# Expert weights in runs of 16 KB per partition: a changed order of features and hidden units in a mixture-of-experts kernel

## The chip, the cores and the metric

One core of one Trainium2 chip runs the whole program. The metric is the time of one execution on the device in microseconds (us); before the change it is 1592.47 us, the median of three runs.

## What is computed

256 tokens of 1024 features go through two blocks. The first mixes tokens (a recurrent RWKV half and an attention half), adds the result to its input, normalises the sum and sends every token to 4 of 32 experts. The second block mixes again and ends in a plain feed-forward network. The change is in the expert layer and in what feeds it; cut to that, the reference is:

```python
x = x + gate1 * (concat([y_rwkv, y_moba]) @ w_out)
h = rms_norm(x, norm2_g) * (1.0 + scale2) + shift2
logits = h @ w_router + b_router
top_val, top_idx = lax.top_k(logits, TOP_K)
weights = softmax(top_val)
...
gu = xb @ w_gate_up[e] + b_gate_up[e]
gate = jnp.minimum(gu[:, :D_FF], SWIGLU_LIMIT)
up = jnp.clip(gu[:, D_FF:], -SWIGLU_LIMIT, SWIGLU_LIMIT)
act = (up + 1.0) * gate * jax.nn.sigmoid(SWIGLU_ALPHA * gate)
y = act @ w_down[e] + b_down[e]
...
x = x + gate2 * segment_sum(y * weight, token)
```

`xb` are the tokens of expert `e`. All of it is float32. An expert's weights are 1024 x 2048 (`w_gate_up`) and 1024 x 1024 (`w_down`) numbers, 12.58 MB; the 32 experts have 403 MB of the 505 MB that the kernel moves. Both products sum over an index, the feature in the first and the hidden unit in the second, and a sum can be taken in any order of its index as long as both factors have the same order.

## The kernel before

**The stream of weights.** All large weights come through one DMA queue, SyncE's (SP), in chunks of 2 MB: one DMA each, into a slot of 128 partitions x 16 KB (`stream`, L105). `issue` (L1021) sends an expert's six chunks, four of `w_gate_up` and two of `w_down`, in the order of use. There are nine slots (three in `ring`, two lent to the first block at first, two each in `ring2` and `ring3`), so a chunk can be sent when the one nine places ahead of it has been used up. In a gate-and-up chunk a partition holds rows `p` and `128 + p` of a pair of groups of 128 features, two runs of 8 KB; in a down chunk it holds four rows, four runs of 4 KB.

**An expert.** `gather` (L1066) makes the input of two experts at a time with 32 products of `xm`, the sum after attention, and a one-hot matrix: `xe[:, k]` holds features `128k` to `128k + 127` on its 128 partitions, 64 slots for tokens per expert. `gate_up` (L1104) runs 32 products of 512 columns (L1117, into `pg` and `pu`), with the 64 tokens as the stationary operand and the weights as the moving one. Four VectorE operations and one of ScalarE (L1120 to L1124) then make `act` (tile `u`): 128 partitions (64 tokens, two halves of the hidden units) x 512. `down` (L1127) transposes `act` in four blocks of 128 columns on TensorE (L1133, tile `at`; the block of `act` is the stationary operand), ScalarE copies the result (L1134), and 16 products (L1139, `py`) multiply it with the down weights. Between the last product of `gate_up` and the first of `down` TensorE has nothing else to do in the experts but for pieces of `gather`, of `combine` (L1149, tile `cb`) and biases that the scheduler put there.

**Ahead of the experts.** `phase1` loads the router's weights `wr` (L593), makes the columns `sc2` and `sh2` (the gain and the shift of the norm's output, feature by feature) from rows `r1` by the four small products of `ada_col` (L293, tile `adac`) and three VectorE operations (L597 to L599), adds what the shift is worth to the router's bias (L602) and folds the gain into `wr` (L604, GpSimd). When the last products with `w_out` are done, the sum `xm` is made in four pieces of 512 features (L871 and L872: two halves `a` of the tokens, two halves `c` of the features), `choose` (L888) transposes it (L897, tile `x1t`), computes the logits (L906) and the mask, `rank` (L919) places the tokens in the experts' slots, and GpSimd copies `xm` to `x1` (L880), the running sum to which the experts add.

The order of instructions on each engine is a scheduler's, made from the program's order and its own costs; it can move an instruction when another one's shape changes.

Of the kernel before, what the change touches and what calls it, by code (L numbers as in the profile page):

```python
# [15 lines left out]
OP = mybir.AluOpType  # L16
# [7 lines left out]
# plain PSUM banks before the experts; buffers of the RWKV and of the stick-breaking attention; how many experts  # L24
# before the last one the memory tokens come in
NP, B4, NZ, ME = 4, 5, 5, 12

# columns of the packed per-feature vectors
# [14 lines left out]
# columns of the constants (they depend on shapes alone)  # L43
# [48 lines left out]
class Kernel:  # L92
# [11 lines left out]
    # ---- weights stream: one order, one queue, a ring of slots  # L104
# [8 lines left out]
    def split(self, pool, src, n, name, eng):  # L113
        """src = hi + lo exactly, each in float32r"""
        hi = pool.tile([128, n], F32R, tag=name + "h", name=name + "h")
        lo = pool.tile([128, n], F32R, tag=name + "l", name=name + "l")
        self.nc.scalar.activation(hi, src, AF.Copy)  # L117
        eng.tensor_tensor(lo, src, hi.bitcast(F32), op=OP.subtract)  # L118
        return hi, lo
# [21 lines left out]
    def setup(self):  # L141
# [9 lines left out]
        # what is not needed past the experts  # L151
        self.xe = ExitStack()
        cp = self.pool("cpe", es=self.xe)
        # x after the attention, its scale per token, and the norm's gain and shift with the modulation, per feature
# [28 lines left out]
    def rsqrt(self, out, src, eps=None, scale=1.0, refine=None):  # L183
        """(src * scale + eps) ** -0.5; with a pool to take temporaries from, one Newton step more"""
# [25 lines left out]
    # ================================================================ first block, before the experts  # L210
    def expert_bias(self, pool):
        """the gate and up biases as three exact bfloat16 parts, on 3 x 32 partitions"""
# [11 lines left out]
    def phase1(self):  # L224
# [9 lines left out]
        # ---- modulation rows: silu(c) @ w_ada + b_ada; the i-th 512 columns add up on the partitions i mod 32  # L234
# [7 lines left out]
        # two slots of the stream that are at first lent to the RWKV and the MoBA  # L242
# [24 lines left out]
        def gate_rows():  # L267
            """rows 4, 5, 10 and 11, for the gates: partition by partition, the bias on one of them"""
# [14 lines left out]
        def gate_bc(q):  # L283
            """a row of a gate on every partition"""
# [4 lines left out]
        def ada_col(r, i0):  # L289
            """rows i0..i0+3 as columns [feature, (row, 128 features)]"""  # L290
# [6 lines left out]
        # ---- x over its root mean square, transposed  # L297
# [29 lines left out]
        # ---- h = rms(x) * g1 * (1 + scale1) + shift1, transposed, as hi + lo  # L327
# [19 lines left out]
        # ---- projections  # L347
# [10 lines left out]
        def dense_T(src, ncols, tiles, consume):  # L358
            """features on partitions; tiles: (first column, columns) of the chunk; two to a bank"""
# [13 lines left out]
        def dense_N(src, consume, then=lambda: None):  # L373
            """tokens on partitions, 512 columns"""
# [21 lines left out]
        def shift_mix(dst, ps, m, mi):  # L396
            """p + (shift(p) - p) * mu"""
# [45 lines left out]
        # ---- RWKV, element by element: decays inside chunks of 64 steps, scaled keys and receptances  # L443
# [9 lines left out]
        for g in ((0, 2), (2, 4)):  # L453
# [3 lines left out]
            # k * k_k over its norm per head  # L457
# [10 lines left out]
            # k * (1 + (a - 1) * k_a)  # L468
# [18 lines left out]
        # ---- RWKV, chunk by chunk: two chunks of 64 steps side by side, eight heads  # L487
# [10 lines left out]
        def pairs(lhs, rhs, tt, name):  # L498
            """per head, [step of lhs, step of rhs]; even heads, then odd ones"""
# [8 lines left out]
        def sub(s):  # L508
            """superchunk s: everything that needs neither the inverse nor the state"""
# [11 lines left out]
            # (I - L)^T of every 16 steps, kept as [row, head, column of the block]  # L521
# [4 lines left out]
        def invert(s, r):  # L526
            """(I - L)^T of every 16 steps: column r times row r of L^T goes to the columns after r"""
# [22 lines left out]
        # ---- MoBA projections (one block, so plain causal attention with ALiBi)  # L550
# [38 lines left out]
        # ---- the router's weights with the gain and the scale of its input folded in, and what its shift adds  # L589
        wr = p1.tile([128, 8, NE], F32, tag="wr", name="wr")  # L590
        cvec = self.W[:, 0]
        with tc.issue_after(self.last_dma):
            nc.sync.dma_start(wr, A["w_router"].rearrange("(k p) e -> p k e", p=128))  # L593
            nc.sync.dma_start(cvec, A["b_router"].partition_broadcast(128))
        pv = ada_col(r1, 6)
        sc2, sh2 = self.sc2, self.sh2
        DVE.tensor_scalar(ic(sc2), pv[:, 2:4], 1.0, None, op0=OP.add)  # L597
        DVE.tensor_tensor(sc2, sc2, self.v("g2"), op=OP.mult)
        DVE.tensor_copy(ic(sh2), pv[:, 0:2])  # L599
# [12 lines left out]
        def sub2(s):  # L612
# [3 lines left out]
            for n, src in (("v", vT), ("a", aT), ("b", bT), ("k", ktT)):  # L616
                if n in ("b", "k"):
                    # decayed to the end of the chunk
# [24 lines left out]
            # what values and keys of the same chunk add to outputs and states  # L643
# [54 lines left out]
        for s in range(2):  # L698
# [32 lines left out]
            # receptance with the decayed keys' corrections folded in; outputs that the state has no part in  # L731
# [17 lines left out]
        # ---- MoBA attention, head by head  # L749
# [21 lines left out]
        def moba_out(hd):  # L771
# [4 lines left out]
            # [key, query]: keys 0..127 for all queries, then keys 128..255 for the last 128  # L776
# [20 lines left out]
        # ---- from here on the stream has more room  # L797
# [10 lines left out]
        # ---- normalised per head, bonus, gate  # L808
        eN = ExitStack()
        pc = right("pc", eN)  # L810
        for s in range(2):
# [11 lines left out]
            # meanwhile what it is multiplied by, and what is added  # L823
# [13 lines left out]
        # ---- x + (y @ w_out) * gate1  # L837
        po = [[self.psum("wo") for _ in range(2)] for _ in range(2)]

        def w_out(ks):  # L840
            """a k after the other; of the last two the first tokens first"""
# [742 lines left out]
```

## Time and profile before

| what | value |
|---|---|
| runs | 1592.47, 1597.8, 1590.65 us (median 1592.47) |
| profiled execution: span | 1590.6 us |
| profiled execution: own time | not given apart; the span lies 1.9 us below the median of the runs |
| TensorE (PE) busy | 1449.3 us, 91% |
| VectorE (DVE), ScalarE (ACT), GpSimd (POOL) busy | 37%, 25%, 13% |
| DMA | 505.15 MB in 115061 packets |
| experts: first product to last | 284 to about 1255 us of the span |

The page gives busy time per engine; the stage views give the same for stretches of the span, with the clock that the throttle granted to TensorE (PEclk, 1.00 is 2.4 GHz and 0.5 is 1.2 GHz), the mean busy share of 16 DMA engines (which can come out a little over 1) and GB/s. A timeline row has start, duration, engine, line, operation, tile written <- tiles read, shape, and in brackets the idle time before it with what ended it. SPq is the DMA queue of SyncE: a duration there is that of issuing, not of the transfer.

### The profile page before, as it was taken

What the parts mean: (1) busy time and instruction counts of PE and PEld (TensorE: products, weight loads), DVE (VectorE), ACT (ScalarE), POOL (GpSimd) and SP (SyncE); (2) the same over time, 40 slices, a digit from 0 to 9 for tenths busy, and PEclk for the clock granted to TensorE, in tenths of its full rate; (3) what the DMA queues carried; (4) which work ended last, traced back from release to release, by engine and by line L of the source; (5) the groups of instructions that cost most, each with busy time, mean ns of one, the idle gap of its engine ahead of it and who ended that gap; (6) DMA issues with size and microseconds to landing.
All of it is one profiled execution on the core that took longest, in us unless ns stands there. A gap on an engine that the chain in (4) does not pass through costs nothing. (4 is left out here: it accounts for less than half of the span.)

```text
span 1590.6 us, 19145 instructions
## 1 busy us (share of the span) xinstructions
PE 1449.3 (91%) x7818; PEld 813.4 (51%) x7818; DVE 591.2 (37%) x1177; ACT 395.1 (25%) x767; POOL 212.6 (13%) x190
## 2 busy tenths in 40 slices
PE   5999998999999989988998989999989899899996
PEld 2976876333333323323333334433333497699995
DVE  2576877232122222221222122222221345555455
ACT  4862344110000000000001011110010366455553
POOL 1243751000000000000000000000000233252221
PEclk9999999999999999999999999999999999989998
DMA  9734747899999999999999997999999451535540
GB/s 337 251 120 170 280 170 288 340 417 416 418 416 416 418 418 415 419 418 415 418 418 415 397 409 319 411 416 416 418 417 414 154 208 54 195 123 180 191 159 27
DMA packets 115061, 505.15 MB, mean 318 GB/s; under 512 B 5548, under 2 KB 6572, under 8 KB 82168
## 3 DMA queue, kind: packets, MB, share of 16 engines
q1 hardware_dynamic: 114792, 503.74, 79.9%
q8 instruction: 63, 1.03, 0.3%
q14 instruction: 30, 0.25, 0.0%
q0 software_dynamic: 176, 0.14, 0.0%
HBM read 502.81 MB, written 1.05 MB: 317 GB/s over the span
## 5 line engine op out<-in xcount | busy, mean ns | idle before, releaser
L1139 PE MATMUL py<-w,at 128*64 128x512 f32 x1024 | 265.0, 669 | 22.0 <-ACT at L1134 21.8
L1117 PE MATMUL pg<-w,xe 128*64 128x512 f32 x1024 | 267.7, 598 | 0.0
L1117 PE MATMUL pu<-w,xe 128*64 128x512 f32 x1024 | 264.9, 592 | 0.0
L1121 ACT ACTIVATE sg<-g 128x512 f32<-128x512 f32 (+1 forms) x33 | 20.2, 616 | 601.6 <-DVE g L1120 601.6
L1139 PEld LDWEIGHTS py<-w,at 128*64 128x64 f32 x1024 | 77.4, 153 | 175.7 <-issue 141.6
L1146 DVE TENSOR_TENSOR y<-py,gate 64x512 f32<-64x512 f32 x64 | 44.1, 688 | 304.4 <-PE py L1139 303.7
L1117 PEld LDWEIGHTS pu<-w,xe 128*64 128x64 f32 x1024 | 74.1, 137 | 146.7 <-issue 146.6
L117 ACT ACTIVATE w3h<-w 128x512 fp32r<-128x512 f32 x184 | 115.2, 631 | 109.1 <-PE d L1275 57.6
L1117 PEld LDWEIGHTS pg<-w,xe 128*64 128x64 f32 x1024 | 70.9, 137 | 135.0 <-issue 130.2
L118 DVE TENSOR_TENSOR w3l<-w,w3h 128x512 fp32r<-128x512 f32 x132 | 94.2, 719 | 115.7 <-ACT w3h L117 111.0
L1120 DVE TENSOR_SCALAR g<-pg 128x512 f32<-128x512 f32 (+1 forms) x33 | 22.2, 675 | 295.4 <-PE pg L1117 295.4
L118 POOL TENSOR_TENSOR w3l<-w,w3h 128x512 fp32r<-128x512 f32 x52 | 67.4, 1301 | 432.1 <-ACT w3h L117 420.9
L1274 PE MATMUL d<-xh,w3h 128*128 128x256 f32 x352 | 100.5, 288 | 0.9 <-ACT xh L1261 0.9
L1210 POOL TENSOR_TENSOR wml<-w,wml 128x512 fp32r<-128x512 f32 x4 | 5.2, 1293 | 718.5 <-ACT wml L1209 718.5
L1275 PE MATMUL d<-xl,w3h 128*128 128x256 f32 x352 | 100.8, 287 | 0.1
L1276 PE MATMUL d<-xh,w3l 128*128 128x256 f32 x352 | 100.2, 286 | 0.0
L1133 PE MATMUL at<-ca,u 128*128 128x128 f32 x128 | 23.5, 313 | 63.8 <-DVE u L1124 63.8
L1083 PEld LDWEIGHTS ga<-s,xm 128*128 128x128 f32 x512 | 62.3, 197 | 28.2 <-issue 26.5
L1083 PE MATMUL ga<-s,xm 128*128 128x128 f32 x512 | 69.8, 288 | 1.2 <-DVE s L1073 1.2
L1274 PEld LDWEIGHTS d<-xh,w3h 128*128 128x128 f32 x352 | 68.4, 196 | 1.6 <-ACT xh L1261 1.3
L1275 PEld LDWEIGHTS d<-xl,w3h 128*128 128x128 f32 x352 | 68.4, 194 | 0.9 <-DVE xl L1263 0.6
L1276 PEld LDWEIGHTS d<-xh,w3l 128*128 128x128 f32 x352 | 68.2, 194 | 0.0
(421 smaller groups left out, 2100.6 us busy)
## 6 DMA issues: line engine op xcount, KB each, us to landing
w<-w_gate_up SPq DMA_DIRECT2D x128, 2048.0 KB, 16.7
w<-w_down SPq DMA_DIRECT2D x71, 2048.0 KB, 17.6
w<-w_ada SPq DMA_DIRECT2D x12, 2048.0 KB, 9.2
w<-w_up SPq DMA_DIRECT2D x8, 2048.0 KB, 7.5
w<-w_in SPq DMA_DIRECT2D x6, 2048.0 KB, 11.4
w<-w_in_sb SPq DMA_DIRECT2D x5, 2048.0 KB, 10.3
w<-w_out SPq DMA_DIRECT2D x4, 2048.0 KB, 7.7
w<-w_mem_kv SPq DMA_DIRECT2D x1, 2048.0 KB, 12.0
```

Of the source, the lines that this page charges most:

```text
L117: self.nc.scalar.activation(hi, src, AF.Copy)
L118: eng.tensor_tensor(lo, src, hi.bitcast(F32), op=OP.subtract)
L1083: PE.matmul(ps[:, k * 128:(k + 1) * 128], xm[:, a, (kk + k) * 128:(kk + k + 1) * 128], s[:, a], start=a == 0, stop=a == 1, skip_group_chec ...
L1117: PE.matmul(p[64 * h:64 * h + 64, :], xe[:, k], w[:, k % 2, c:c + 512], start=False, stop=k == 7)
L1120: DVE.tensor_scalar(g[:, c], pg[:, c], 7.0, None, op0=OP.min)
L1121: ACT.activation(s[:, c], g[:, c], AF.Sigmoid, scale=1.702)
L1133: PE.transpose(ps[:, j * 128:(j + 1) * 128], act[:, j * 128:(j + 1) * 128], ident)
L1139: PE.matmul(py[64 * h:64 * h + 64, :], at[:, j, c], ws[c][:, j, h * 512:(h + 1) * 512], start=c == 0 and j == 0, stop=c == 1 and j == 3)
L1146: DVE.tensor_tensor(st[e & ~1][2][r, hs], py[64 * h:64 * h + 64], self.gate2[64 * h:64 * h + 64, hs], op=OP.mult)
L1274: PE.matmul(o, wh[:, ws], xh[:, k], start=k == 0 and i % 2 == 0, stop=False, skip_group_check=True)
L1275: PE.matmul(o, wh[:, ws], xl[:, k], start=False, stop=False, skip_group_check=True)
L1276: PE.matmul(o, wl[:, ws], xh[:, k], start=False, stop=k == 7, skip_group_check=True)
```

## The change

1. **Weights.** A chunk of `w_gate_up` now holds, on partition `p`, two whole groups of the rows `8p` to `8p + 7`: feature `8p + k` stands where feature `128k + p` stood, and the two rows of a chunk are neighbours in memory, one run of 16 KB. A chunk of `w_down` holds on partition `p` the rows `4p` to `4p + 3` of its half, one run of 16 KB.
2. **Features.** All that is multiplied with these rows follows: the router's weights `wr`, the columns `sc2` and `sh2` (16 products of 64 x 2 with every eighth column of `r1` as the stationary operand, in place of four of 128 x 4; the norm's gain comes by a DMA of its own), and `xm`, which VectorE now writes with a step of 512 bytes between neighbours. GpSimd undoes the order when it copies `xm` to `x1`. Each half `c` of the features now has columns in all eight blocks of `xm`.
3. **Hidden units.** The four transposes of an expert read every fourth column of `act`, a step of 16 bytes, in place of 128 neighbours. For the last expert, which works in two parts, the elementwise operations are strided too.
4. **The path for an overfull expert** (`overflow`), which isn't taken in these runs, is addressed anew.

The rest of the diff takes out comments.

```diff
         with tc.issue_after(self.last_dma):
-            nc.sync.dma_start(wr, A["w_router"].rearrange("(k p) e -> p k e", p=128))
+            nc.sync.dma_start(wr, A["w_router"].rearrange("(p k) e -> p k e", p=128))
+            nc.sync.dma_start(sc2, A["norm2_g"].rearrange("(p k) -> p k", p=128))
             nc.sync.dma_start(cvec, A["b_router"].partition_broadcast(128))
-        pv = ada_col(r1, 6)
-        sc2, sh2 = self.sc2, self.sh2
-        DVE.tensor_scalar(ic(sc2), pv[:, 2:4], 1.0, None, op0=OP.add)
-        DVE.tensor_tensor(sc2, sc2, self.v("g2"), op=OP.mult)
-        DVE.tensor_copy(ic(sh2), pv[:, 0:2])
+
+        ps = self.psum("adac")
+        for i in range(2):
+            for k in range(8):
+                PE.matmul(ps[64 * i:64 * i + 64, 2 * k:2 * k + 2], r1[:, k:512:8], self.k("sel32")[:, 6 + i:10:2],
+                          start=True, stop=True, skip_group_check=True)
+        pv = ps[:, 0:16].rearrange("p (k i) -> p i k", i=2)
+        DVE.scalar_tensor_tensor(sc2, pv[:, 1], 1.0, sc2, op0=OP.add, op1=OP.mult)
+        DVE.tensor_copy(sh2, pv[:, 0])
...
+        pk = lambda t: t.rearrange("t (p k) -> t p k", k=8)
+        xp = lambda a: xm[:, a].rearrange("t (k p) -> t p k", k=8)
         for a in range(2):
             for c in range(2):
...
-                DVE.tensor_tensor(xm[:, a, cs], x1[:, a, cs], t, op=OP.add)
+                DVE.tensor_tensor(xp(a)[:, 64 * c:64 * c + 64], pk(x1[:, a, cs]), pk(t), op=OP.add)
...
-            POOL.tensor_copy(x1[:, a], xm[:, a])
+            POOL.tensor_copy(pk(x1[:, a]), xp(a))
...
             if j < 4:
-                g = A["w_gate_up"][e].rearrange("(k p) f -> p k f", p=128)
+                g = A["w_gate_up"][e].rearrange("(p k) f -> p k f", p=128)
                 w = self.stream(g[:, 2 * j:2 * j + 2], 2, 2048, pool)
             else:
-                d = A["w_down"][e].rearrange("(k p) f -> p k f", p=128)
-                w = self.stream(d[:, 4 * j - 16:4 * j - 12], 4, 1024, pool, 4 if i == 6 * self.ne - 1 else 1)
+                d = A["w_down"][e].rearrange("(c p j) f -> c p j f", c=2, p=128)
+                w = self.stream(d[j - 4], 4, 1024, pool, 4 if i == 6 * self.ne - 1 else 1)
...
-            return [slice(0, 256), slice(256, 512)] if e == ne - 1 else [slice(0, 512)]
+            return [slice(0, 2), slice(2, 4)] if e == ne - 1 else [slice(0, 4)]
+
+        cut = lambda t, c: t.rearrange("p (q j) -> p q j", j=4)[:, :, c] if c != slice(0, 4) else t
...
-                js = slice(c.start // 128, c.stop // 128)
-                for j in range(js.start, js.stop):
-                    PE.transpose(ps[:, j * 128:(j + 1) * 128], act[:, j * 128:(j + 1) * 128], ident)
-                ACT.activation(at[:, js], ps[:, c].rearrange("p (j h s) -> p j h s", h=2, s=64), AF.Copy)
+                for j in range(c.start, c.stop):
+                    PE.transpose(ps[:, j * 128:(j + 1) * 128], act[:, j:512:4], ident)
+                ACT.activation(at[:, c], ps[:, c.start * 128:c.stop * 128].rearrange("p (j h s) -> p j h s", h=2, s=64),
+                               AF.Copy)
```

**What moves.** In the experts and after them every engine has the same instructions in the same order as before; what differs there are shapes. The first piece is of SyncE's queue at the place where the router's weights and the first chunks of the experts are sent; the difference reads:

```order
-L593 DMA wr<-w_router 128x8x32
-L594 DMA W<-b_router 128x32
+L594 DMA wr<-w_router 128x256
+L595 DMA sc_71<-norm_g 128x8
+L596 DMA W<-b_router 128x32
 L110 DMA w<-w_out 128x8x512
-L110 DMA w<-w_gate_up 128x2x2048
+L110 DMA w<-w_gate_up 128x4096
 L110 DMA w<-w_out 128x8x512
```

Nothing changes places; one small DMA is added and each chunk has one run per partition. The second piece is TensorE where the last products with `w_out` (tile `wo`) end and the experts are chosen. Before:

```order
L854 MATMUL wo<-wsl,yoh 128x512 x2
L897 MATMUL x1t<-ca,xm 128x128 x8
L906 MATMUL lg<-wr,x1T 128x32 x4
L897 MATMUL x1t<-ca,xm 128x128 x4
L906 MATMUL lg<-wr,x1T 128x32 x4
L897 MATMUL x1t<-ca,xm 128x128 x4
L906 MATMUL lg<-wr,x1T 128x32 x8
```

And with the change:

```order
L860 MATMUL wo<-wsl,yoh 128x512 x2
L906 MATMUL x1t<-ca,xm 128x128 x8
L915 MATMUL lg<-wr,x1T 128x32 x8
L906 MATMUL x1t<-ca,xm 128x128 x8
L915 MATMUL lg<-wr,x1T 128x32 x4
L934 MATMUL rk<-mask,ca 128x32
L915 MATMUL lg<-wr,x1T 128x32 x4
```

The transposes of a half of the tokens now stand together, and all the logits of the first half stand ahead of the transposes of the second. The third piece is VectorE at the same place, before:

```order
L871 TENSOR_TENSOR gx<-wo,gate 128x512
L872 TENSOR_TENSOR xm<-x_65,gx 128x512
L871 TENSOR_TENSOR gx<-wo,gate 128x512 x2
L872 TENSOR_TENSOR xm<-x_65,gx 128x512
L902 COPY x1T<-x1t 128x512
```

And with the change:

```order
L880 TENSOR_TENSOR gx<-wo,gate 128x512
L881 TENSOR_TENSOR xm<-x_65,gx 128x64x8
L880 TENSOR_TENSOR gx<-wo,gate 128x512 x2
L881 TENSOR_TENSOR xm<-x_65,gx 128x64x8 x2
L880 TENSOR_TENSOR gx<-wo,gate 128x512
```

The third piece of the sum moved ahead of the copy of the first transposes (`x1T`), which follows behind the fifth row of the second fence.

## Rows read from the trace of the kernel before

**Rows 1.** The page: span, and TensorE's busy time and share

```profile
span 1590.6 us, 19145 instructions
PE 1449.3 (91%) x7818; PEld 813.4 (51%) x7818; DVE 591.2 (37%) x1177; ACT 395.1 (25%) x767; POOL 212.6 (13%) x190
```

**Rows 2.** Waits of TensorE, 284 to 1255 us: total us, times, longest

```profile
PE at L1133 <- DVE u L1124: 63.8, 25, 2.9
PE py L1139 <- ACT at L1134: 21.8, 31, 1.2
PE cb L1155 <- DVE y L1146: 0.8, 1, 0.8
...
```

**Rows 3.** Waits of SyncE's DMA queue, 400 to 900 us

```profile
SPq L110 <- PE pu L1117: 214.5, 54, 6.8
SPq L110 <- PE py L1139: 137.7, 32, 10.2
SPq L110 <- PE at L1133: 68.6, 11, 7.0
```

**Rows 4.** Timeline of SyncE's queue, 705 to 745 us, and tile w from 700 to 762

```profile
706.48 3.80 SPq L110 DMA_DIRECT2D w<-w_down  x2
...
DMA to landing us min/median/max: 16.2/19.7/21.8
```

**Rows 5.** Stages: length, busy us (instructions) by engine, PEclk, DMA share, GB/s

```profile
284.05:448.37 164.32, 157.42 (x754) 61.20 (x752) 43.88 (x93) 15.56 (x30) 0.00 (x0) 0.98 0.99 403
448.37:573.14 124.77, 111.60 (x502) 41.91 (x500) 27.99 (x56) 8.69 (x18) 0.00 (x0) 0.93 1.02 417
```

**Rows 6.** The same view for 8 us of down chunks and of gate-and-up chunks

```profile
721.00:729.00 8.00, 8.00 (x44) 3.69 (x44) 1.38 (x2) 0.00 (x0) 0.00 (x0) 1.00 1.03 413
736.00:744.00 8.00, 7.45 (x36) 2.40 (x35) 3.07 (x10) 0.96 (x3) 0.00 (x0) 1.00 1.01 420
```

**Rows 7.** Timeline of TensorE, 710.5 to 720 us: an even expert

```profile
712.28 1.03 PE L1117 MATMUL pu<-w,xe 128*64 128x512 f32 x4
715.71 0.63 PE L1133 MATMUL at<-ca,u 128*128 128x128 f32 x4 [2.40 <-DVE u L1124]
717.02 3.22 PE L1139 MATMUL py<-w,at 128*64 128x512 f32 x14 [0.69 <-ACT at L1134]
```

**Rows 8.** Timeline of TensorE, 741 to 762 us: the odd expert that follows

```profile
746.30 1.09 PE L1133 MATMUL at<-ca,u 128*128 128x128 f32 x4 [2.85 <-DVE u L1124]
748.08 5.85 PE L1139 MATMUL py<-w,at 128*64 128x512 f32 x16 [0.69 <-ACT at L1134]
...
754.20 3.60 PE L1139 MATMUL py<-w,at 128*64 128x512 f32 x16
```

**Rows 9.** Timeline of TensorE, 619.9 to 626 us: an odd expert at the full clock

```profile
619.94 1.03 PE L1117 MATMUL pu<-w,xe 128*64 128x512 f32 x4
623.82 0.63 PE L1133 MATMUL at<-ca,u 128*128 128x128 f32 x4 [2.85 <-DVE u L1124]
625.14 1.08 PE L1139 MATMUL py<-w,at 128*64 128x512 f32 x4 [0.69 <-ACT at L1134]
```

**Rows 10.** All transposes of `act`: loads and products, ns min/median/max

```profile
L1133 PEld LDWEIGHTS at<-ca,u x128: 138/141/231, 300.3 to 1248.0; 128*128 128x128 f32 x128
L1133 PE MATMUL at<-ca,u x128: 272/273/448, 300.3 to 1248.1; 128*128 128x128 f32 x128
```

**Rows 11.** The page's groups: down products, busy us and mean ns

```profile
L1139 PE MATMUL py<-w,at 128*64 128x512 f32 x1024 | 265.0, 669 | 22.0 <-ACT at L1134 21.8
```

**Rows 12.** Timelines of TensorE and VectorE, 262 to 278 us: choosing the experts

```profile
265.08 0.66 PE L897 MATMUL x1t<-ca,xm 128*128 128x128 f32 x4
266.91 0.66 PE L897 MATMUL x1t<-ca,xm 128*128 128x128 f32 x4 [1.17 <-DVE xm L872]
...
264.33 0.69 DVE L872 TENSOR_TENSOR xm<-x,gx 128x512 f32<-128x512 f32 x1
```

**Rows 13.** Timeline of TensorE, 160 to 190 us: the products that make the columns

```profile
162.72 0.95 PE L293 MATMUL adac<-ca,ar 128*128 128x4 f32 x8
```

More of the change, by code (lines that the diff above doesn't have):

```diff
@@ L590, in phase1 @@
         wr = p1.tile([128, 8, NE], F32, tag="wr", name="wr")
+        sc2, sh2 = self.sc2, self.sh2
         cvec = self.W[:, 0]
         with tc.issue_after(self.last_dma):
-            nc.sync.dma_start(wr, A["w_router"].rearrange("(k p) e -> p k e", p=128))
+            nc.sync.dma_start(wr, A["w_router"].rearrange("(p k) e -> p k e", p=128))
+            nc.sync.dma_start(sc2, A["norm2_g"].rearrange("(p k) -> p k", p=128))
             nc.sync.dma_start(cvec, A["b_router"].partition_broadcast(128))
-        pv = ada_col(r1, 6)
-        sc2, sh2 = self.sc2, self.sh2
-        DVE.tensor_scalar(ic(sc2), pv[:, 2:4], 1.0, None, op0=OP.add)
-        DVE.tensor_tensor(sc2, sc2, self.v("g2"), op=OP.mult)
-        DVE.tensor_copy(ic(sh2), pv[:, 0:2])
+        ps = self.psum("adac")
[6 more added lines that the diff above has]
+        DVE.tensor_copy(sh2, pv[:, 0])
         ps = self.psum("cv")
@@ L972, in turned, with weights @@
                                 DVE.tensor_copy(t8[:, k], ps[:, 0:128])
-                    def weights(name, rows, cols):
+                    def weights(rows, cols):
                         w = pool.tile([128, 512], F32, tag="w", name="wo", bufs=2)
-                        nc.sync.dma_start(w, A[name][ds(e, 1), rows, cols].rearrange("e p f -> p (e f)"))
+                        nc.sync.dma_start(w, rows[ds(e, 1), :, cols].rearrange("e p f -> p (e f)"))
                         return w
@@ L986, in overflow @@
                                     c = slice(j * D + i * 512, j * D + (i + 1) * 512)
-                                    w = weights("w_gate_up", slice(k * 128, (k + 1) * 128), c)
+                                    w = weights(A["w_gate_up"].rearrange("e (p k) f -> e k p f", k=8)[:, k], c)
                                     PE.matmul(pg[j], t8[:, k], w, start=k == 0, stop=k == 7)
@@ L1004, in overflow @@
                             for i in range(2):
-                                w = weights("w_down", slice(k * 128, (k + 1) * 128), slice(i * 512, (i + 1) * 512))
+                                w = weights(A["w_down"][:, k * 128:(k + 1) * 128], slice(i * 512, (i + 1) * 512))
                                 PE.matmul(py[i], t8[:, k], w, start=k == 0, stop=k == 7)
@@ L1119, in gate_up @@
             for c in cuts(e):
-                DVE.tensor_scalar(g[:, c], pg[:, c], 7.0, None, op0=OP.min)
-                ACT.activation(s[:, c], g[:, c], AF.Sigmoid, scale=1.702)
-                DVE.tensor_scalar(u[:, c], pu[:, c], 7.0, -7.0, op0=OP.min, op1=OP.max)
-                DVE.scalar_tensor_tensor(u[:, c], u[:, c], 1.0, g[:, c], op0=OP.add, op1=OP.mult)
-                DVE.tensor_tensor(u[:, c], u[:, c], s[:, c], op=OP.mult)
+                DVE.tensor_scalar(cut(g, c), cut(pg, c), 7.0, None, op0=OP.min)
+                ACT.activation(cut(s, c), cut(g, c), AF.Sigmoid, scale=1.702)
+                DVE.tensor_scalar(cut(u, c), cut(pu, c), 7.0, -7.0, op0=OP.min, op1=OP.max)
+                DVE.scalar_tensor_tensor(cut(u, c), cut(u, c), 1.0, cut(g, c), op0=OP.add, op1=OP.mult)
+                DVE.tensor_tensor(cut(u, c), cut(u, c), cut(s, c), op=OP.mult)
             return u
```

## The prediction

> **What bounds the kernel now.** I read the page first: TensorE is busy for 91% of the span [rows 1], so it, or what it waits for, sets the time. The change is aimed at the weights' transfers, so the next question is whether TensorE ever waits for one. The list of its waits through all experts says no [rows 2]: the two entries of weight, 63.8 and 21.8 us, name VectorE and ScalarE, which make `act` and copy its transposes, and no entry names a DMA (the two left out, of 0.5 us each, name ScalarE).
>
> The queue's own waits show the other side [rows 3]: it stands until TensorE has used up a slot. One chunk followed through [rows 4]: two down chunks are sent between 706.48 and 710.28; the slowest landing in that stretch took 21.8 us, so both lie there by 732.1. They are multiplied from 748.08 on [rows 8], 16 us later, and that product waited for ScalarE. The stages say how narrow this is [rows 5]: from 448 us on four experts take 124.77 us, 31.2 us each, while 12.58 MB at the 417 GB/s of that stage take 30.2. The stream's DMA share is about 1 and it is still not the bound: TensorE is slower by 1 us per expert. In the first six experts, which live on chunks loaded beforehand, TensorE needs 27.4 us each (164.32 / 6).
>
> What TensorE loses per expert is the gap between the last product of `gate_up` and the first of `down`. In an even expert [rows 7] it is 2.40 us for VectorE, 0.63 for four transposes, 0.69 for ScalarE: 3.72. In an odd one VectorE takes 2.85 [rows 9], which makes 4.17. Behind the gap the clock can fall: the sixteen products that follow took 5.85 us in one odd expert [rows 8], where sixteen at full speed took 3.60, and its transposes 1.09 instead of 0.63. These are the two levels of 2.4 and 1.2 GHz; the engine had stood nearly idle for some 4 us before. Over all experts the down products took 265.0 us [rows 11]; 64 times 3.60 are 230.4, so 34.6 us are lost, at 2.25 (5.85 - 3.60) each about 15 experts that fall to the lower clock.
>
> **Longer runs: 0 us.** Down chunks move at 413 GB/s, gate-and-up chunks at 420 [rows 6], so 4 KB runs cost 5.08 us per 2.097 MB and 8 KB runs 4.99: a doubling from 4 to 8 KB is worth 0.085. Runs of 16 KB are in no row. If each further doubling is worth half of the last, four chunks save 0.043 each and two save 0.128, 0.43 us per expert, 13.6 us in all; if it is worth as much as the last, 22; at least nothing. None of it reaches the end while TensorE finds its chunks 16 us early: the queue only stands longer for slots. I take 0. If that cover were gone, the 13.6 would count (second rival).
>
> **Strided transposes: 15.2 us.** Each expert's four transposes now load their stationary block with a step of 16 bytes. Four took 0.63 us and a single product of them lasts 0.273 [rows 7, 10], so one follows the other after (0.63 - 0.273) / 3 = 0.119 us. No row has a load with such a step. The lower bound is nothing: the load, 0.138 us, runs beside the product before it [rows 10]. For the upper one I take it that a load costs by the stretch that it spans: 512 numbers instead of 128, four times, 0.476 us per step. A gain is excluded, since the same numbers are read from more places. Between ends so far apart I take the geometric middle, a doubling: 4 x 0.119 = 0.48 us per expert, all of it inside the gap, which nothing covers. 32 x 0.48 = 15.2 us, between 0 and 46.
>
> The Trainium skill, SBUF — State Buffer, on Door 1, states that memory is read in lines of 16 bytes, that consecutive accesses to one line run at full bandwidth and that each access that crosses to a new line pays a penalty. It speaks against this change: every number read is now on a new line. By it alone the first rival would be out; no run here shows it yet.
>
> **The longer gap: 16.3 us.** With 0.48 us more an even expert's gap is 4.20 us, as long as an odd one's today. A gap of 4.17 comes today with either level [rows 8, 9]; one of 3.72 kept the full clock [rows 7]. The first six experts have other products in the gap, which leaves 13 even ones. I let half of them, six, fall: 6 x (2.25 + 0.46) = 16.3 us; the bounds are none and all 13, 35 us.
>
> **Elementwise operations and the copy of the transposes: 0.** For 31 experts their operands are as before; the last one's are strided, a few operations of below 1 us each.
>
> **Ahead of the experts: 1 us.** The sum `xm` is written with a step of 512 bytes; a piece takes 0.69 us now [rows 12], four pieces, so at twice the price 2.8 us more, at least nothing. TensorE's first transposes ran at 265.08, before the second piece; now they need both pieces and can start where the second four did, at 266.91, so 1.8 us later. But the end of this stage hangs on the second half's last piece, which doesn't move by that, so the two don't add up to more than 2.8. The small products for the columns go from four (eight entries, two passes each, 0.95 us [rows 13]) to sixteen, at most 2.9 us more at the same price each, at least nothing where TensorE waits there anyway; two VectorE operations take the place of three. The new DMA is queued behind the router's weights on SyncE, with the router's bias and the first chunks behind it; its 4 KB are nothing next to 2 MB chunks. GpSimd's copy back to `x1` is not needed before the experts add to it. From 0 to 5.7 us in all; I take 1, since each price is an upper one and the work sits in chains that mostly wait for something else.
>
> **Sum.** 0 + 15.2 + 16.3 + 0 + 1 = 32.5 us on a profiled span of 1590.6, or 1623.1. The span lies 1.9 us below the median of the runs (the profiled execution has no time of its own), so the forecast is **1625 us**.
>
> **Rivals.**
>
> *Strided loads are free* (0.35). The load is hidden behind the product before it; then the gap, the clock and the total stay: 1590.6 + 1 + 1.9 = 1593.5 us, not slower. For it: a load takes 0.138 us, near the step of 0.119, yet with two at work at once the products don't wait. Against it: load and step are so close that a load of twice the length could no longer hide. It decides if a strided load stays under about 0.15 us per step: four times 0.03 us in 32 experts are 4 us, under what can be measured. That the change doesn't do what it says belongs here too: if the runs in memory came out as packets no longer than before, nothing is gained by the stream, and the time would be the same unless the transposes cost.
>
> *The stream is the bound after all* (0.08). The DMA share of 1.02 speaks for it, and that an expert takes only 1 us more than its transfers. Then longer runs give 13.6 us: 1590.6 - 13.6 + 1 + 1.9 = 1580 us, faster. Against it stands that in 971 us TensorE waited for no chunk [rows 2]. Together with 0.02 for something else of that sign this is the whole chance of faster.
>
> *The new order in memory slows the stream* (0.03). A gate-and-up chunk reads 16 KB on each partition from rows that start 64 KB apart; before, neighbouring partitions' runs stood next to each other. It becomes the bound when six chunks take over 31.2 us, at a mean rate below 12.58 / 31.2 = 403 GB/s, which is just under today's 417. If gate-and-up fell to 350 GB/s, four chunks would take 24.0 us instead of 20.0, an expert 34.2, and 26 experts at 3.0 us more each give 1590.6 + 78 + 1.9 = 1670 us. No row shows a slower rate for a larger distance.
>
> The Trainium skill, DMA: Bandwidth & Descriptors, on latency and other measured facts, gives for rows 512 KiB apart 207 GB/s, nearly the full rate of 214 there, and a fall only from 2 MiB on. Its table holds no 64 KB; by it this rival would not come about.
>
> **How the numbers follow.** The chance of the forecast case, strided loads that cost, with a clock that falls more often, is 0.52; the rivals have 0.35, 0.08 and 0.03, something else 0.02 (faster). About 0.5%, 8 us, is what a measurement of this kernel tells from no change. Faster by over 0.5% is 0.08 + 0.02 = 0.10; within 0.5% 0.35; slower 0.52 + 0.03 = 0.55. The range goes down to the second case, 1593.5 with 5.5 us for the scatter of runs and prices, 1588, which leaves out the faster tenth. Upward it takes the forecast with all 13 even experts at the lower clock, 1590.6 + 15.2 + 35 + 1 + 1.9 = 1643.7, and ends at 1643; what lies above (dearer loads, a slower stream) has less than a tenth.
>
> **What would show it right or wrong.** In the changed kernel's timeline four transposes of `act` should take 0.63 + 3 x 0.119, about 1.0 us at the full clock, and their loads more than 0.141; if they still take 0.63 the first rival holds. The even gap should go from 3.72 to 4.2, and the down products from 265.0 to about 279 us. The stream should have packets of 16 KB, so well below the present number in all; its queue should still wait for TensorE, and TensorE's waits should still name no transfer. If they name one, the second or third rival is at work: at a rate above 417 GB/s the second, below 403 the third. I should be wrong altogether if the experts took fewer than 31.2 us each without any wait for a DMA having gone.

## The result, and the profile after

The changed kernel takes 1615.82 us (median of four runs, 1609.05 to 1618.75) where the kernel before took 1591.56 beside it (four runs, 1590.5 to 1597.8): ratio 1.0132, 95% interval 1.0095 to 1.017. It is slower by 1.3%, 21 us by the ratio. The forecast was 1625, slower, with a range of 1588 to 1643. The parts of the sum are another matter.

The page of the changed kernel, with the lines that answer to [rows 1] and [rows 11], and its line of packets (115061 before):

```profile
span 1613.0 us, 19195 instructions
PE 1465.6 (91%) x7842; PEld 826.7 (51%) x7842; DVE 598.2 (37%) x1176; ACT 394.8 (24%) x767; POOL 215.0 (13%) x190
...
DMA packets 73734, 505.16 MB, mean 313 GB/s; under 512 B 4669, under 2 KB 5821, under 8 KB 49161
...
L1150 PE MATMUL py<-w,at 128*64 128x512 f32 x1024 | 267.2, 674 | 21.9 <-ACT at L1144 21.8
```

The packets did become fewer, so the change does what it says; the down products took 267.2 us, hardly more than 265.0. TensorE's waits through its experts, 298 to 1275 us, which answer to [rows 2]:

```profile
PE at L1143 <- DVE u L1135: 63.8, 25, 2.9
PE py L1150 <- ACT at L1144: 21.8, 31, 1.2
PE cb L1166 <- DVE y L1157: 0.8, 1, 0.8
```

The queue's from 400 to 900 us, as [rows 3]:

```profile
SPq L110 <- PE pu L1128: 242.6, 63, 6.8
SPq L110 <- PE py L1150: 215.8, 33, 10.5
```

TensorE's two large waits are those of before, 63.8 and 21.8 us. It still waits for no chunk, and the queue still for TensorE. The stream itself got faster: the stage from 448 us on moved 428 GB/s where [rows 5] has 417, and then, with its slots full, less (columns as there):

```profile
448.00:573.00 125.00, 114.68 (x540) 45.17 (x538) 30.22 (x64) 9.24 (x19) 0.00 (x0) 0.96 1.01 428
573.00:696.00 123.00, 109.73 (x490) 41.28 (x488) 28.20 (x56) 8.67 (x18) 0.00 (x0) 0.93 0.99 409
```

All loads and products of the transposes, as [rows 10]:

```profile
L1143 PEld LDWEIGHTS at<-ca,u x128: 195/212/230, 314.6 to 1267.7; 128*128 128x128 f32 x128
L1143 PE MATMUL at<-ca,u x128: 272/285/462, 314.6 to 1267.8; 128*128 128x128 f32 x128
```

One even expert of TensorE's timeline, as [rows 7]:

```profile
734.47 0.72 PE L1143 MATMUL at<-ca,u 128*128 128x128 f32 x4 [2.41 <-DVE u L1135]
735.88 3.65 PE L1150 MATMUL py<-w,at 128*64 128x512 f32 x16 [0.69 <-ACT at L1144]
```

A load with the step takes 0.212 us instead of 0.141, but four transposes only 0.72 instead of 0.63.

So where did the time go? The last pair of products with `w_out` starts 8.05 us later than before (272.59 instead of 264.54), the first product of the experts 14.35 later (298.40 instead of 284.05), the last down product 19.7 later (1274.7 instead of 1255.0), and the span is 22.4 us longer. Ahead of the experts 14.4 us are lost, in them 5.3, behind them 2.7. The first 8.05 us are lost around the new small products. TensorE's timeline there, as [rows 13]:

```profile
163.81 3.55 PE L601 MATMUL adac<-ca,ar 128*64 128x2 f32 x32
167.29 0.47 PE L632 MATMUL tr<-ca,dc 128*128 128x128 f32 x1
```

The same stretch in steps of 2 us, with the granted clock third from the end (columns as in [rows 5]):

```profile
166.00:168.00 2.00, 2.00 (x14) 1.76 (x14) 0.00 (x0) 0.00 (x0) 0.00 (x0) 0.76 1.04 384
168.00:170.00 2.00, 2.00 (x9) 1.65 (x8) 0.20 (x1) 0.00 (x0) 0.00 (x0) 0.50 1.06 390
...
176.00:178.00 2.00, 2.00 (x17) 1.88 (x15) 2.00 (x5) 0.00 (x0) 2.00 (x2) 0.68 0.00 0
```

The block starts 1.1 us later than the old one (163.81 instead of 162.72) and takes 2.6 us more, and from about 167 to 177 us the granted clock is 0.50, that is 1.2 GHz, where the kernel before had 1.00 in this stretch; that leaves some 4.4 us for the clock. The second loss is the choosing. The timelines of TensorE and VectorE, as [rows 12]:

```profile
275.56 1.33 PE L906 MATMUL x1t<-ca,xm 128*128 128x128 f32 x8 [2.35 <-DVE xm L881]
277.60 3.62 PE L915 MATMUL lg<-wr,x1T 128*128 128x32 f32 x16 [0.71 <-DVE nwt L194]
...
272.38 1.07 DVE L881 TENSOR_TENSOR xm<-x,gx 128x512 f32<-128x512 f32 x1
```

And the stretch in steps of 4 us:

```profile
272.00:276.00 4.00, 1.65 (x10) 1.11 (x9) 3.97 (x6) 0.47 (x1) 0.43 (x1) 1.00 1.00 426
276.00:280.00 4.00, 3.29 (x18) 2.88 (x16) 3.88 (x9) 2.60 (x6) 3.04 (x2) 0.53 1.05 446
...
292.00:296.00 4.00, 4.00 (x20) 4.00 (x20) 1.62 (x2) 0.48 (x2) 0.00 (x0) 0.50 0.08 24
```

TensorE waits 2.35 us for both pieces of `xm`, where the kernel before waited 1.17, a piece costs VectorE 1.07 us instead of 0.69, and then the products run at 1.2 GHz until 296 us. The kernel before falls to the lower clock in the choosing too, but later in it and for some 7 us instead of some 20:

```profile
272.00:276.00 4.00, 2.31 (x14) 2.07 (x14) 3.12 (x27) 0.64 (x2) 0.00 (x0) 0.84 1.02 420
276.00:280.00 4.00, 2.78 (x13) 2.81 (x14) 2.25 (x10) 0.00 (x0) 0.59 (x1) 0.50 1.02 424
280.00:284.00 4.00, 4.00 (x31) 3.83 (x32) 1.49 (x6) 1.65 (x4) 0.00 (x0) 0.81 0.61 217
```

### The profile page after: what moved, and what is told of

Same layout as the page of the kernel before. It is cut to its first block, busy times and chain, and to the rows that moved or that the text cites. A ratio compares the mean times of both kernels' runs of the same rounds, so it can differ in the third digit from the quotient of the medians.

```text
span 1613.0 us, 19195 instructions
## 1 busy us (share of the span) xinstructions
PE 1465.6 (91%) x7842; PEld 826.7 (51%) x7842; DVE 598.2 (37%) x1176; ACT 394.8 (24%) x767; POOL 215.0 (13%) x190
## 5 line engine op out<-in xcount | busy, mean ns | idle before, releaser
L1150 PE MATMUL py<-w,at 128*64 128x512 f32 x1024 | 267.2, 674 | 21.9 <-ACT at L1144 21.8
L1143 PE MATMUL at<-ca,u 128*128 128x128 f32 x128 | 24.9, 323 | 63.8 <-DVE u L1135 63.8
L1092 PEld LDWEIGHTS ga<-s,xm 128*128 128x128 f32 x512 | 63.1, 199 | 28.2 <-issue 26.5
```

The lines of the kernel that those rows point to most:

```text
L1092: PE.matmul(ps[:, k * 128:(k + 1) * 128], xm[:, a, (kk + k) * 128:(kk + k + 1) * 128], s[:, a], start=a == 0, stop=a == 1, skip_group_chec ...
L1150: PE.matmul(py[64 * h:64 * h + 64, :], at[:, j, c], ws[c][:, j, h * 512:(h + 1) * 512], start=c == 0 and j == 0, stop=c == 1 and j == 3)
```

## The experiments

Two theories stood against each other. **A**: most of the loss arises ahead of the experts, from the order of the features, in good part through the clock. **B**, the prediction's: strided transposes and the longer gap. Each kernel below was timed against the kernel before on its chip in five rounds; a distance in us is the ratio's, times 1592.

### e1 and e2: one half of the change alone

e1 is the kernel before with the edits of the third part of the change and of the down chunks; e2 is the changed kernel with just these undone:

```diff
-                d = A["w_down"][e].rearrange("(c p j) f -> c p j f", c=2, p=128)
-                w = self.stream(d[j - 4], 4, 1024, pool, 4 if i == 6 * self.ne - 1 else 1)
+                d = A["w_down"][e].rearrange("(k p) f -> p k f", p=128)
+                w = self.stream(d[:, 4 * j - 16:4 * j - 12], 4, 1024, pool, 4 if i == 6 * self.ne - 1 else 1)
...
-                    PE.transpose(ps[:, j * 128:(j + 1) * 128], act[:, j:512:4], ident)
+                    PE.transpose(ps[:, j * 128:(j + 1) * 128], act[:, j * 128:(j + 1) * 128], ident)
```

> The kernel before with the hidden units' part of the change alone (down chunks in runs of 16 KB, transposes of act with a step of 16 bytes). Theory A (most of the loss arises ahead of the experts, from the order of the features): first product of the experts at 284 us as before, four transposes in some 0.72 us instead of 0.63, total 3 to 8 us above before (ratio 1.002 to 1.005). Theory B, that of the prediction (strided transposes and the lower clock behind a longer gap): 15 to 30 us above before (1.010 to 1.019).

> The changed kernel with the hidden units' part undone: down chunks in four runs of 4 KB, transposes of neighbouring columns; the features keep their new order and gate-and-up chunks their runs of 16 KB. Theory A: first product of the experts near 298 us, 14 to 18 us above before (ratio 1.009 to 1.011). Theory B: first product near 285, total 0 to 3 us above before.

Measured: e1 1.0049 (1.0022 to 1.0077), 7.8 us above before; e2 1.0103 (1.0059 to 1.0147), 16.4 us above. Together, 24 us, they give the change's 21 within the intervals. In e1 four transposes take 0.72 us and the down products 267.3, in e2 the experts start at 298.9 us. The features cost two thirds, as A has it, and e1's list of TensorE's waits names no chunk. In e1's trace the experts take 5.4 us more than before (286.7 to 1263.1 us): 32 x 0.09 = 2.9 are the transposes themselves, 2.3 the down products, whose clock e10 tests. Another 2.7 us lie ahead of the experts, in the choosing, which e1 leaves as it was: here the clock fell earlier than in the kernel before.

The experts' stage parts the kernels cleanly. From the first product of the experts to the last down product it takes 971 to 972 us in the traces without a step and with the gap as it was (the kernel before, e2, and e7 below), and 975 to 983 in the five with a step (the changed kernel, e1, and e3, e4 and e8 below); their down products take 264.9 to 265.5 us and 265.9 to 272.4.

### e7: the sixteen small products added to the kernel before

```diff
         pv = ada_col(r1, 6)
+        ps = self.psum("adac")
+        for i in range(2):
+            for k in range(8):
+                PE.matmul(ps[64 * i:64 * i + 64, 2 * k:2 * k + 2], r1[:, k:512:8], self.k("sel32")[:, 6 + i:10:2],
+                          start=True, stop=True, skip_group_check=True)
+        DVE.tensor_copy(self.sh2, ps[:, 0:8])
```

> The kernel before with the sixteen small products of the changed kernel added behind its own four, their result unused (one VectorE copy). If they cost what the changed kernel's trace shows at their place (3.55 us of products and a lower clock behind them): the first transposes of the choosing start 6 to 9 us later, total 5 to 9 us above before (ratio 1.003 to 1.006). If only their own time counts: 3 to 4 us.

Measured: 1.0042 (1.0018 to 1.0066), 6.7 us, where the products themselves take 3.55. The clock falls while they run, near their end in the changed kernel (the timeline has them from 166.31 to 169.9; steps of 2 us):

```profile
166.00:168.00 2.00, 2.00 (x20) 1.98 (x21) 1.91 (x7) 0.37 (x1) 0.00 (x0) 0.93 1.06 388
168.00:170.00 2.00, 2.00 (x21) 1.99 (x20) 0.11 (x1) 0.00 (x0) 0.00 (x0) 0.50 1.04 384
```

The interval reaches down to 3 us, so the traces, not the time, carry the point on the clock. In all five traces with sixteen or, as in e3 next, eight small products at this place the clock falls in them or right behind them; in the other seven it is 1.00 from 160 to 176 us. The first transposes of the choosing start 8.8 us later than in the kernel before, but not all of that is theirs: this execution, the longest of its twelve, has a second fall of the clock, from 190 to 198 us.

### e3: eight products in place of sixteen

```diff
-                PE.matmul(ps[64 * i:64 * i + 64, 2 * k:2 * k + 2], r1[:, k:512:8], self.k("sel32")[:, 6 + i:10:2],
+        r2 = xm[:, 0]
+        DVE.tensor_copy(r2.rearrange("p (k i q) -> p k i q", k=8, i=2),
+                        r1.rearrange("p (q k) -> p k q", k=8)[:, :, None, :].to_broadcast([128, 8, 2, 64]))
...
+            PE.matmul(ps[:, 4 * k:4 * k + 4], r2[:, k * 128:(k + 1) * 128], self.k("sel32")[:, 6:10],
```

> The changed kernel with the sixteen products of 64 x 2 for the columns replaced by eight of 128 x 4 on a copy of the rows that VectorE has put in order (no strided stationary operand). Theory A: the block takes about 1.9 us instead of 3.55, the clock stays at 1.00 behind it, the last products with w_out and all that follows start 5 to 7 us earlier than in the changed kernel, total 5 to 7 us below it (about 1609). If the small products do not matter: no difference to the changed kernel.

A miss: 1.0144 (1.0092 to 1.0196), no better than the changed kernel. The block, from 164.11 us on, did shrink to 1.95 us, but the clock fell all the same (steps of 2 us):

```profile
166.00:168.00 2.00, 2.00 (x10) 1.52 (x9) 0.80 (x2) 0.00 (x0) 0.00 (x0) 0.59 1.03 383
168.00:170.00 2.00, 2.00 (x8) 1.37 (x7) 0.98 (x3) 0.57 (x1) 0.00 (x0) 0.50 1.05 387
```

The experts begin at 294.9 us, 3.5 before the changed kernel's, and in this execution take 6 us more (down products 272.4 us), about as much as that stage differs among the five traces with a step (975 to 983 us). Whether eight products are worth anything stays open within its 8 us of uncertainty.

### e4: the router in the old order

The sum, the transposes, the router's weights and its four small products are as before; GpSimd's copy makes the new order, and e3's eight products stand behind the choosing in the program.

```diff
-                DVE.tensor_tensor(xp(a)[:, 64 * c:64 * c + 64], pk(x1[:, a, cs]), pk(t), op=OP.add)
+                DVE.tensor_tensor(x1[:, a, cs], x1[:, a, cs], t, op=OP.add)
...
-            POOL.tensor_copy(pk(x1[:, a]), xp(a))
+            POOL.tensor_copy(xp(a), pk(x1[:, a]))
```

> The changed kernel with the router in the old order of features: VectorE adds without a step, the transposes, the router's weights and their columns are as before; GpSimd makes the copy in the new order for the experts, and the columns in that order come from eight products that stand behind the choosing. Stream and transposes of act stay as changed. Theory A: first product of the experts at 284 to 287 us, total 4 to 9 us above before, 13 to 17 below the changed kernel. Theory B: within 4 us of the changed kernel.

Measured: 1.0069 (1.0044 to 1.0093), 11 us above before and 10 below the changed kernel: A's direction, a little short of its numbers. The first product of the experts, which A put at 284 to 287 us, comes at 299.0 in its profile. That execution (1612.49 us, median 1605.05) has a fall of the clock of its own from 178 to 198 us, behind the old four products and a wait of 1.55 us for VectorE; the kernel before waits 1.77 us at this place and keeps 1.00.

The choosing, from the last pair of products with `w_out` to the first product of the experts, did not get shorter: 25.1 us here and 25.2 in e9 below, which has the same router. It takes 25.4 to 25.8 in the four traces with the strided sum (the changed kernel, e2, e3 and e6 below) and 19.2 to 22.3 in the six that leave it alone. For the scheduler put the eight products between the logits, here in e9 at the lower clock:

```profile
274.81 1.91 PE L922 MATMUL lg<-wr,x1T 128*128 128x32 f32 x8
276.54 3.55 PE L887 MATMUL adac<-ca,ar 128*128 128x4 f32 x16
```

So e4 shows that the new order ahead of the experts costs some 10 us, but not at which step. How much of the second loss is the dearer sum and how much the new order of TensorE's products stays open; no run parts them.

### e8 and e10: the price of a step, and of the gap

e8 gives the kernel before down chunks of two runs of 8 KB and transposes with a step of 8 bytes; e10 is e1 with the order made by the last VectorE operation, so that the transposes read neighbours. In e10 the two parts of the last expert write over each other, which changes its values and not its work.

```diff
+                d = A["w_down"][e].rearrange("(c J p i) f -> c p J (i f)", c=2, J=2, p=128)
...
+                    PE.transpose(ps[:, j * 128:(j + 1) * 128], act[:, j // 2 * 256 + j % 2:j // 2 * 256 + 256:2], ident)
```

```diff
-                DVE.tensor_tensor(cut(u, c), cut(u, c), cut(s, c), op=OP.mult)
+                jq = lambda t: t.rearrange("p (q j) -> p j q", j=4)[:, c]
+                DVE.tensor_tensor(g.rearrange("p (j q) -> p j q", j=4)[:, c], jq(u), jq(s), op=OP.mult)
...
-                    PE.transpose(ps[:, j * 128:(j + 1) * 128], act[:, j:512:4], ident)
+                    PE.transpose(ps[:, j * 128:(j + 1) * 128], act[:, j * 128:(j + 1) * 128], ident)
```

> The kernel before with down chunks in two runs of 8 KB per partition and transposes of act that read every second column of one half: a step of 8 bytes instead of 16. If a load pays for each line of 16 bytes and needs two reads per line for full speed: loads of 0.14 us as before (0.21 with a step of 16 bytes), total within 3 us of before. If any step costs: loads near 0.21 us, total 5 to 10 us above before as with the step of 16.

> As e1 (hidden units alone), but the last VectorE operation on act puts the units in order, reading with a step of 16 bytes, and the transposes read neighbours again. If e1's loss comes from the loads with a step (0.211 us against 0.141): loads at 0.141 us, total back to within 3 us of before, unless the VectorE operation, which lies in the same gap, gets dearer than its 0.69 us; each 0.1 us there costs 3 us and what the clock adds. If e1's loss came from the order of the down rows in memory: still 5 to 10 us above before.

Measured: e8 1.0043 (1.0017 to 1.0069), 6.8 us above before; e10 1.0153 (1.0119 to 1.0187). The loads of e8:

```profile
L1134 PEld LDWEIGHTS at<-ca,u x128: 194/209/230, 300.4 to 1258.4; 128*128 128x128 f32 x128
```

The loads of e10:

```profile
L1135 PEld LDWEIGHTS at<-ca,g x128: 137/141/231, 301.2 to 1268.3; 128*128 128x128 f32 x128
```

Its last VectorE operation on `act` in the groups of 300 to 1250 us:

```profile
L1127 DVE TENSOR_TENSOR g<-u,sg 128x512 f32<-128x512 f32 x31 | 33.0, 1064 | 2.2 <-DVE u L1125 0.5
```

A step of 8 bytes costs a load as much as one of 16. In e10 the loads are back at 0.141 us, but the VectorE operation takes 1.064 us instead of 0.688. That 0.38 us lies in the same gap: TensorE's waits for VectorE at the transposes are 73.9 us in all (71.4 and 2.5) instead of 63.8, 10 us more, the down products take 274.4 us, 9.4 more, and the total is 24 us above before. A longer gap costs about twice its own length, the rest being the clock. The step's 0.09 us, 2.9 us in all, gave 5.4 in the experts of e1. This is the prediction's mechanism at nearly its own dose. What the loads alone cost e10 does not tell, since the dearer operation covers it.

### e5, e6 and e9: the gap filled

If TensorE's time goes into the gap and the clock behind it, work in the gap should give it back. One product per expert from the seventh on, which reads the first VectorE result of the gap, keeps the scheduler from moving the gather and the combine ahead of it, so that they fall into the gap. e5 is the kernel before with it, e6 the changed kernel, e9 is e4 with it.

```diff
                 DVE.tensor_scalar(g[:, c], pg[:, c], 7.0, None, op0=OP.min)
+                if 6 <= e < ne - 1:
+                    ps = self.psum("fill")
+                    for _ in range(1):
+                        PE.matmul(ps[0:64, :], g[:, 0:64], self.ca[:, 0:512], start=True, stop=True)
```

> The kernel before with the gather of the next two experts and the combine of the last two held in the gap between the up products and the transposes, from the seventh expert on: one extra product per expert, 64 x 512 on the first VectorE result of the gap, keeps the scheduler from moving them ahead. If the gap and the lower clock behind it are what TensorE loses there: down products from 265.0 to about 235 us, an expert in some 28 us of TensorE's time, so that the stream becomes the bound at 30.2 us per expert (12.58 MB at 417 GB/s) and TensorE's waits name chunks for the first time; total 25 to 45 us below the kernel before. If the gap is not the loss: no difference or 11 us slower (26 extra products of 0.43 us).

> The changed kernel with the same extra product. With the stream as the bound the longer runs should now show: 12.58 MB at 428 GB/s are 29.4 us per expert, 0.8 less than with the old runs, so the experts take 15 to 25 us less than in the kernel before with the same product; against that stand the 14 us that the change loses ahead of the experts, so the totals of the two lie within 12 us of each other. If the longer runs are worth nothing even then: 14 to 20 us above the kernel before with the same product.

> The changed stream and transposes with the router in the old order of features, as in e4, and the gap filled as in e6. If the gains add: the stream is the bound at 29.4 us per expert, and the part ahead of the experts takes 5 to 14 us less than in e6: total 1545 to 1555 us, below e5, e6 and the kernel before. If the part ahead of the experts does not matter once the stream is the bound: as e6, 1559.

Measured: e5 1571.87 us, 0.9845 (0.9813 to 0.9878); e6 1558.98 us, 0.9765 (0.9733 to 0.9797); e9 **1549.2 us**, 0.9713 (0.9683 to 0.9742), faster than both kernels. e5 lies 24.7 us below the kernel before, just short of the 25 to 45 expected, and e6 12.9 below e5, where at most 12 were. TensorE's timeline in e5 around one gap:

```profile
696.75 1.07 PE L1124 MATMUL fill<-ca,g 128*64 128x512 f32 x2
697.75 3.70 PE L1159 MATMUL cb<-y,swt 128*128 128x512 f32 x8
701.29 0.60 PE L1137 MATMUL at<-ca,u 128*128 128x128 f32 x4
702.57 3.65 PE L1143 MATMUL py<-w,at 128*64 128x512 f32 x16 [0.69 <-ACT at L1138]
```

TensorE's largest waits in e5, 284 to 1260 us:

```profile
PE pg L1117 <- DMA w<-w_gate_up: 46.9, 38, 1.8
PE py L1143 <- ACT at L1138: 20.6, 30, 0.7
PE at L1137 <- DVE u L1128: 4.3, 2, 2.3
```

And a stage of it (columns as in [rows 5]):

```profile
450.00:700.00 250.00, 232.99 (x1099) 88.28 (x1096) 62.24 (x120) 18.55 (x37) 0.00 (x0) 1.00 1.02 417
```

The wait for VectorE falls from 63.8 to 4.3 us, the clock is 1.00 in the whole stage, the down products take 232.3 us, and for the first time TensorE waits for chunks, 46.9 us. Now the stream is the bound, and e6 shows what the longer runs are worth. The same stage:

```profile
450.00:700.00 250.00, 240.95 (x1162) 94.69 (x1158) 65.31 (x131) 21.38 (x43) 0.00 (x0) 1.00 1.01 428
```

428 GB/s instead of 417, and TensorE's waits for gate-and-up chunks fall from 46.9 to 26.5 us; from the first product of the experts to the last down product e6 takes 921.1 us (300.1 to 1221.2) and e5 941.6 (287.3 to 1228.9). That is 20.5 us for the change where the stream binds, against 12.8 us that it loses ahead of the experts in this pair; TensorE's waits for all chunks, down chunks with them, fall by about as much, from 49.3 to 28.6 us. e9 starts its experts at 293.2 us, 6.9 before e6, of which 6.5 are there at the last products with `w_out` already, and keeps the faster stream.

## Why the prediction came out

The total came out and its parts did not. In the experts 31.5 us were forecast and 5.3 measured in the trace, 26 too much; outside them 1 was forecast and 17.1 measured, 16 too little. That these errors stood on opposite sides and left the time 9 us from the forecast, inside the range, is luck.

- **Longer runs, 0 us: right.** The stream was covered in the kernel before, and stayed so in the changed one. Where it is not covered, in e6, it is worth 20.5 us, between the two estimates of 13.6 and 22 and near the second: 2.097 MB at 417 and at 428 GB/s differ by 0.13 us per chunk, 0.78 in an expert's six chunks with their eight doublings, so a doubling, at 0.10, is worth about as much as the 0.085 of the last one.
- **Strided transposes, 15.2 us forecast, 2.9 measured.** The failed step is the geometric middle between ends far apart. The load did get longer, by half (0.141 to 0.212 us) and not to double, and most of it is still hidden beside the product before it: three steps of 0.03 us where four of 0.119 were taken (the prediction's own sign, about 1.0 us for four transposes, counts three).
- **The longer gap, 16.3 us forecast, 2.2 measured** in the changed kernel's down products (267.2 less 265.0), and 0.9 to 7.4 in the five traces with a step. The mechanism held, as e10 and e5 show from both sides; its size hung on the gap's 0.48 us, of which 0.09 came.
- **Ahead of the experts, 1 us forecast, 14.4 measured.** This is the step that was wrong in kind. The small products' own price was bounded well (2.6 measured, at most 2.9), and so was VectorE's (1.07 against 0.69 us for a piece). But the text weighed the clock for the gap in the experts alone. Here too TensorE had little to do, at 2-column products and in a wait of 2.35 us, and everything for some 10 and 20 us behind ran at 1.2 GHz, where the kernel before had nothing and some 7. A part of the 14.4 can be scatter: e1 and e5, which leave this part alone, begin their experts 2.7 and 3.3 us later than the kernel before. The claim that the wait and the dearer pieces "don't add up to more than 2.8" left this out.
- **Behind the experts, not forecast, 2.7 us.** This isn't the change's. No kernel here touches that part, and it takes 334.5 to 339.5 us in the twelve traces (335.6 before, 338.3 with the change), the longest in e5 and e7, which are the kernel before with products added elsewhere.

The first rival (strided loads are free) was nearly true of the loads and still gave no 1593, because of the part ahead of the experts. The second (the stream is the bound) was false for this kernel and true for e5. The third, a slower stream, did not come. On the Trainium skill's lines of 16 bytes (SBUF — State Buffer, Door 1): the trace agrees that a step costs a load, 0.212 against 0.141 us, but with a step of 8 bytes, where two of the numbers read lie on each line, the load costs the same 0.209, so here the penalty does not go by the number of lines.

## What to carry to other kernels

A faster transfer is worth nothing while its wait is not the last to end; find the engine that binds, fill its gap, and measure the transfer again: here the same change cost 1.3% before that and gained 0.8% after it. Price every gap and every run of tiny products on TensorE with the clock behind it, in each stage that an edit touches, not only in the one that it is meant for, and read the clock's part from several traces: the same choosing took 19.2 to 22.3 us. Where an order must be changed, don't give it to the engine that the next one waits for: in e10 VectorE's dearer operation cost 24 us, the strided loads that it saved 7.8 in e1. GpSimd's copy is off the path (in e9 it ends at 276.2 us, and the gather that reads it starts at 285.5), but in e4 and e9 the small products moved too, so what it is worth by itself isn't shown.

## What was not expected of the hardware

In or right behind two blocks of small products, 3.55 us of 64 x 2 and 1.95 us of 128 x 4, the clock fell for 7 to 10 us although TensorE was busy nearly all the time in the profile's rows (2.00 of 2.00 us, once 1.89 in e3). And a load of 128 columns with any step tried, 8 or 16 bytes, took 0.21 us in place of 0.14.
